# Two-layer macaron encoder on one core: the instruction order laid down with the builder's other machine model

## The chip, the core and the metric

The kernel runs on one core of one Trainium2 chip. Its time is that of one execution on the device in microseconds (us); several executions give a median. A core has five engines that each work through their own list of instructions strictly in order, and that wait for each other only where one needs the other's data or a buffer that it frees: PE (TensorE, matmuls, with its weight loads shown apart as PEld), DVE (VectorE), ACT (ScalarE), POOL (GpSimd) and SP (SyncE, which here only issues DMAs).

## What is computed

The reference applies two layers to x of 512 positions and 1024 channels, in fp32, and a last RMSNorm:

```python
x = x + 0.5 * swiglu(rmsnorm(x), gate1, up1, down1)       # hidden width 2816
h = rmsnorm(x); p = h @ w_in                               # 2048 columns
# A, 256 columns: centred means over 2, 4, 8, 16 positions minus the token, a map per group
# B, 256 columns: real part of a 2-D DFT over (positions, group channels), a linear map
# C, q, k, v of 4 heads: softmax(q1 k1) - lam * softmax(q2 k2), with a distance penalty,
#    times v, RMSNorm per head
x = x + concat(A, B, C) @ w_out
x = x + 0.5 * swiglu(rmsnorm(x), gate2, up2, down2)
```

## The kernel before

x lies in SBUF as eight tiles of 128 channels x 512 positions. Every fp32 factor is taken apart into a rounded part hi (ACT, L103) and the rest lo (DVE, in some steps POOL, L104); a product is three matmuls: hi with hi, and hi with lo both ways (L107 to L109 in general, L386 to L388 in the feed-forward products).

**Weights.** They come in blocks of 128 x 1024 by DMAs that SP issues (L158) into seven buffers named st. Some blocks are sums of two blocks of the weight matrix; there POOL issues a second DMA that adds to what lies in the buffer (L160), and another after a block has been used, which turns the buffer into the next sum (L175). `produce` makes hi and lo of a block, in four buffers each, and `operand` hands them out, three blocks ahead.

**Feed-forward block.** It has 11 units in three chunks of 4, 4 and 3. A unit computes two gate and two up tiles of 128 hidden channels with seven products instead of eight, over halves of the positions, accumulated in four PSUM banks qe, qa, qb, qg: `head` (qe, qa, then a copy q1 of qa, L395), `middle` (qb, qg; then y, v, w on DVE, L402 to L404; then qa again) and `tail` (qg again, qe again, then the SiLU products). In the program the tail of a unit stands behind the head of the next. A product is 24 matmuls. At a chunk's end come eight down products (banks dn), each of 24 (18) matmuls of 512 columns, added to x (L452). The norm's squares (ACT, L274), their sum (POOL, the last on DVE, L278) and the sum over channels on PE (bank ss, L254 and L255) run beside the first unit and are needed by its last step.

**Mixer.** Its steps are named in a list, ORDER (L44 to L48): `P` and `E` project q and k of a head and scale and split them (tq, tk at L474 and L475; qs, kh, kl at L480 to L485), `S01` is the scores of head 0 for the positions of block 1, `V0` and `V1` the values, `T` transposes, `X` weighs the values (bank AV), `Y` finishes a head, `GH` is a channel map of the Fourier part, `PL` the pooling part's map. A score step: two matmul pairs give scores in PSUM (S), DVE adds the distance penalty and takes the maximum in one instruction (L499), a small DVE instruction scales the maximum to nb (L503), ACT takes the exponential with its row sum (L504), DVE inverts the sums (L506) and scales (L507), one of three engines scales the first softmax (L509 is ACT's, L511 DVE's, L513 POOL's), and DVE subtracts the second (L514).

**What sets the order.** The program text gives only the order in which instructions are handed to the builder. The builder lays down each engine's list itself: it runs through the program with a model of the machine, takes what the model says is ready, and writes every engine's instructions in the order in which the model starts them. Priorities follow the program's order. All semaphores and waits come after that. The model's answer is thus fixed in the kernel: at run time an instruction whose inputs are late blocks everything behind it on its engine.

## Time and profile before

| | |
|---|---|
| median of 3 runs | 1875.59 us (1872.73 to 1879.64) |
| profiled execution | 1877.81 us |
| its span, first to last instruction | 1876.0 us |
| mean granted TensorE clock | 0.982 |
| HBM read | 261.09 MB, 140 GB/s over the span |
| DMA engines' share, POOL's queue and SP's | 29.1% and 27.7% |

One execution is profiled. A row of the timeline gives the start in us, the duration, the engine, the line, the operation, the tile written and those read, and in brackets how long the engine had been idle and who ended that. Matmuls overlap: a row's duration is longer than the distance to the next row. The granted clock is the share of full speed at which TensorE was allowed to run.

### The profile page before, as it was taken

To read this page: it belongs to the slowest core of one execution; us is meant where nothing else is said; L and a number is where in the kernel's file an instruction comes from. 1 tells how busy PE (TensorE), PEld (TensorE's weight loads), DVE (VectorE), ACT (ScalarE), POOL (GpSimd) and SP (SyncE) were. 2 spreads that over 40 slices of the span, in tenths; PEclk is the share of its full clock that TensorE was granted. 3 is DMA by queue.
4 is the path that set the end of the run, shared out by engine and by line. 5 is a ranking of instruction groups with operands and counts; after the bars stand their busy time and mean duration, and the time that the engine had idled before them with its cause. 6 is when DMAs were issued, how large, how long until landed. Compare 5 with 4: busy or idle time off the path is not lost.

```text
span 1876.0 us, 27955 instructions
## 1 busy us (share of the span) xinstructions
PE 1774.7 (95%) x11225; PEld 1603.5 (85%) x11225; DVE 1360.3 (73%) x1956; ACT 851.9 (45%) x1189; POOL 320.6 (17%) x282
## 2 busy tenths in 40 slices
PE   5899999999879999999999999999996989999997
PEld 4898989987668999989989899898775889899896
DVE  6675765789779874855798567478987897567474
ACT  6342533448545442534555234243773554244243
POOL 3101101032322101101031010113232220010101
PEclk9899999999989999999999999999998999999998
DMA  8666867532213866857678577573322267586561
GB/s 231 150 169 137 204 165 156 138 120 85 65 42 78 188 161 147 211 151 155 161 154 195 142 167 189 129 180 124 93 71 56 65 140 197 128 193 177 127 166 45
DMA packets 76738, 265.01 MB, mean 141 GB/s; under 512 B 8640, under 2 KB 10688, under 8 KB 76608
## 3 DMA queue, kind: packets, MB, share of 16 engines
q0 software_dynamic: 25344, 92.29, 29.1%
q1 hardware_dynamic: 48096, 167.25, 27.7%
q10 hardware_dynamic: 3168, 3.68, 0.7%
q8 instruction: 88, 1.44, 0.3%
q14 instruction: 42, 0.34, 0.1%
HBM read 261.09 MB, written 2.10 MB: 140 GB/s over the span
## 4 chain that ended last, share of the span: by engine, by line
PE 69%; DVE 12%; issue 7%; DMA 5%; ACT 5%; POOL 2%; SPq 0%; DVEq 0%; ACTq 0%; POOLq 0%
PE dn L107 7%; PE dn L108 7%; PE dn L109 7%; DMA st<-in_gu 5%; PE qg L386 4%; PE qg L387 4%; PE qg L388 4%; PE qe L386 3%; PE qe L387 3%; PE qe L388 3%; PE qa L388 3%; PE qa L386 3%; PE qa L387 3%; DVE lo L104 2%; ACT hi L103 2%
## 5 line engine op out<-in xcount | busy, mean ns | idle before, releaser
L103 ACT ACTIVATE hi<-st 128x1024 fp32r<-128x1024 f32 (+2 forms) x455 | 469.2, 1036 | 668.0 <-PE dn L108 214.8
L104 DVE TENSOR_TENSOR lo<-st,hi 128x1024 fp32r<-128x1024 f32 (+2 forms) x423 | 511.5, 1213 | 179.4 <-ACT hi L103 178.3
L108 PE MATMUL dn<-al,hi 128*128 128x512 f32 x704 | 274.6, 390 | 0.0
L109 PE MATMUL dn<-ah,lo 128*128 128x512 f32 x704 | 274.1, 389 | 0.0
L107 PE MATMUL dn<-ah,hi 128*128 128x512 f32 x704 | 272.1, 392 | 0.8
L175 POOL DMA_DIRECT2D st<-in_gu x132 | 120.7, 914 | 680.3 <-DVE lo L104 606.2
L386 PE MATMUL qe<-xh,hi 128*128 128x256 f32 x704 | 203.3, 289 | 20.0 <-ACT hi L103 10.3
L386 PE MATMUL qg<-xh,hi 128*128 128x256 f32 x704 | 201.3, 286 | 8.1 <-DVE w L404 7.7
L387 PE MATMUL qe<-xh,lo 128*128 128x256 f32 x704 | 202.6, 288 | 2.2 <-DVE lo L104 2.2
L388 PE MATMUL qe<-xl,hi 128*128 128x256 f32 x704 | 202.1, 287 | 1.8 <-DVE xl L104 1.8
L387 PE MATMUL qg<-xh,lo 128*128 128x256 f32 x704 | 200.8, 285 | 2.8 <-DVE lo L104 2.8
L388 PE MATMUL qg<-xl,hi 128*128 128x256 f32 x704 | 200.6, 285 | 0.0
L452 DVE SCALAR_TENSOR_TENSOR x<-dn,x 128x512 f32<-128x512 f32 x96 | 66.1, 689 | 163.2 <-PE dn L109 163.2
L107 PEld LDWEIGHTS dn<-ah,hi 128*128 128x128 f32 x704 | 131.3, 188 | 33.1 <-ACT ah L103 7.1
L386 PEld LDWEIGHTS qe<-xh,hi 128*128 128x128 f32 x704 | 137.9, 196 | 23.9 <-ACT hi L103 16.0
L108 PEld LDWEIGHTS dn<-al,hi 128*128 128x128 f32 x704 | 132.2, 188 | 29.0 <-DVE al L104 2.4
L109 PEld LDWEIGHTS dn<-ah,lo 128*128 128x128 f32 x704 | 132.2, 188 | 26.8
L386 PEld LDWEIGHTS qg<-xh,hi 128*128 128x128 f32 x704 | 136.4, 194 | 9.4 <-DVE w L404 7.6
L387 PEld LDWEIGHTS qe<-xh,lo 128*128 128x128 f32 x704 | 137.9, 196 | 4.0 <-DVE lo L104 3.1
L388 PEld LDWEIGHTS qe<-xl,hi 128*128 128x128 f32 x704 | 138.0, 196 | 2.4 <-DVE xl L104 2.0
L387 PEld LDWEIGHTS qg<-xh,lo 128*128 128x128 f32 x704 | 136.5, 194 | 3.0 <-DVE lo L104 3.0
L388 PEld LDWEIGHTS qg<-xl,hi 128*128 128x128 f32 x704 | 136.6, 194 | 0.0
(252 smaller groups left out, 3979.1 us busy)
## 6 DMA issues: line engine op xcount, KB each, us to landing
st<-in_gu SPq DMA_DIRECT2D x176, 512.0 KB, 4.5
st<-in_gu POOLq DMA_DIRECT2D x176, 512.0 KB, 5.6
st<-in_dn SPq DMA_DIRECT2D x64, 512.0 KB, 4.3
st<-in_dn SPq DMA_DIRECT2D x32, 384.0 KB, 3.3
st<-in_qk SPq DMA_DIRECT2D x16, 512.0 KB, 3.6
st<-in_wo SPq DMA_DIRECT2D x16, 512.0 KB, 3.7
st<-in_wv SPq DMA_DIRECT2D x8, 512.0 KB, 3.9
st<-in_wfa SPq DMA_DIRECT2D x8, 512.0 KB, 3.7
```

What stands on the lines that cost most here:

```text
L103: A.activation(hi, src, AF.Copy)
L104: (lo_eng or V).tensor_tensor(lo, src, f(hi), SUB)
L107: T.matmul(o, lh, rh, start=start, stop=False)
L108: T.matmul(o, lh, rl, start=False, stop=False)
L109: T.matmul(o, ll, rh, start=False, stop=stop)
L175: G.dma_start(t[:, 0:w], then, accum_op=ADD)
L386: T.matmul(o, wh[:, s], xh, start=start and p == 0 and z == 0, stop=False, **k)
L387: T.matmul(o, wl[:, s], xh, start=False, stop=False, **k)
L388: T.matmul(o, wh[:, s], xl, start=False, stop=stop and p == NK - 1 and z == 1, **k)
L452: V.scalar_tensor_tensor(X[m], b, 0.5, X[m], MUL, ADD)
```

## The change

One argument where the kernel's context is made:

```diff
@@ -855,7 +855,7 @@
         arrays[f"in_{name}"] = a
         args[name] = nc.dram_tensor(f"in_{name}", a.shape, F32, kind="ExternalInput").ap()
     args["out"] = nc.dram_tensor("out_t", (KT, P, S), F32, kind="ExternalOutput").ap()
-    with _tile.TileContext(nc) as tc:
+    with _tile.TileContext(nc, schedule_with_timeline_sim=True) as tc:
         build(tc, **args)
     r = _run(nc, [arrays], core_ids=[0])
```

The builder then orders the instructions with its other model of the machine, one that has times for queues and transfers. The instructions, their operands and the engine of each stay the same; PE has 11196 rows in both orders and ACT 1142. SP's list does not change at all. On PE, DVE, ACT and POOL many rows move, nearly everywhere. Three places:

ScalarE at the start. xg, xh and xo are parts of the input, hi of a weight block; q is the copy q1, and the rows sq are the norm's squares. Before:

```order
L103 ACTIVATE hi_260<-st_91 128x1024
L103 ACTIVATE xh_242<-xg_223 128x512
L103 ACTIVATE hi_290<-st_102 128x1024
L103 ACTIVATE hi_350<-st_132 128x1024
L395 ACTIVATE q_51_318<-qa_247 128x512
L274 ACTIVATE sq_320<-x_81 128x512
L274 ACTIVATE sq_322<-x_82 128x512
L274 ACTIVATE sq_325<-x_83 128x512
L274 ACTIVATE sq_328<-x_84 128x512
```

And now:

```order
L103 ACTIVATE hi_250<-st_95 128x1024
L103 ACTIVATE xh_242<-xg_223 128x512
L395 ACTIVATE q_51_318<-qa_247 128x512
L274 ACTIVATE sq_320<-x_81 128x512
L274 ACTIVATE sq_322<-x_82 128x512
L274 ACTIVATE sq_325<-x_83 128x512
L274 ACTIVATE sq_328<-x_84 128x512
L274 ACTIVATE sq_331<-x_85 128x512
L274 ACTIVATE sq_334<-x_86 128x512
L274 ACTIVATE sq_337<-x_87 128x512
L274 ACTIVATE sq_340<-x_88 128x512
L103 ACTIVATE hi_255<-st_95 128x1024
```

The squares and q1 stood behind the conversions of five weight blocks (hi_250, further up, to hi_350); now they stand behind one, and the other four follow them. On GpSimd the additions of these squares move in the same way: four of the six stand in one piece now, ahead of a DMA issue that stood between the first two.

VectorE in the score steps of the first mixer, first group (head 0 block 1, head 1 blocks 1 and 3). S0 and S1 are scores, mx maxima, rs the row sums of ACT's exponentials. Before:

```order
L499 ISA sc_334_4033,mx_327_4019<-S1_333_4030,al_104 128x512
L499 ISA mx_327_4019 128x1
L503 TENSOR_SCALAR nb_328_4020<-mx_327_4019 128x1
L499 ISA sc_340_4048,mx_335_4041<-S1_339_4045,al_104 128x512
L499 ISA mx_335_4041 128x1
L506 RECIPROCAL rc_322_4000<-rs_321_3999 128x2
```

And now:

```order
L499 ISA sc_342_4055,mx_335_4041<-S1_341_4052,al_104 128x512
L499 ISA mx_335_4041 128x1
L474 SCALAR_TENSOR_TENSOR tq_343_4063<-pp0_309_3925,y_293_3806 128x512
L475 TENSOR_TENSOR tk_344_4064<-pp1_310_3926,y_293_3806 128x512
L503 TENSOR_SCALAR nb_320_3998<-mx_319_3997 128x1 x2
L503 TENSOR_SCALAR nb_328_4020<-mx_327_4019 128x1 x2
L503 TENSOR_SCALAR nb_336_4042<-mx_335_4041 128x1 x2
L482 TENSOR_TENSOR qs_345_4067<-tq_343_4063,qs_345_4067 64x512
L483 TENSOR_TENSOR kl_347_4069<-tk_344_4064,kh_346_4068 64x512
L506 RECIPROCAL rc_322_4000<-rs_321_3999 128x2
```

The L503 of a tile stood behind the next reduction or the one after; now all six of the group stand behind all six reductions (the first row is the last of them) and behind the two scalings of the next head, and the reciprocals and L507 follow in one piece. The second group has its first four L503 in one piece too.

TensorE where the first down products of the first block meet the next chunk's first unit. dn_1304 is the second down product, dn_1336 and dn_1368 the third and fourth; qe_950 is the last product of a tail. Before:

```order
L388 MATMUL qe_950<-xl_243,hi_1119 128x256
L109 MATMUL dn_1304<-ah_842,lo_1190 128x512
L107 MATMUL dn_1304<-ah_804,hi_1189 128x512
L108 MATMUL dn_1304<-al_805,hi_1189 128x512
L109 MATMUL dn_1304<-ah_804,lo_1190 128x512
L107 MATMUL dn_1304<-ah_1083,hi_1189 128x512
L108 MATMUL dn_1304<-al_1084,hi_1189 128x512
L109 MATMUL dn_1304<-ah_1083,lo_1190 128x512
L107 MATMUL dn_1304<-ah_1045,hi_1189 128x512
L108 MATMUL dn_1304<-al_1046,hi_1189 128x512
L109 MATMUL dn_1304<-ah_1045,lo_1190 128x512
L107 MATMUL dn_1336<-ah_600,hi_1229 128x512
```

And now:

```order
L386 MATMUL qe_950<-xh_242,hi_1119 128x256
L387 MATMUL qe_950<-xh_242,lo_1120 128x256
L388 MATMUL qe_950<-xl_243,hi_1119 128x256
L107 MATMUL dn_1336<-ah_600,hi_1229 128x512
L108 MATMUL dn_1336<-al_601,hi_1229 128x512
L107 MATMUL dn_1368<-ah_600,hi_1267 128x512
L108 MATMUL dn_1368<-al_601,hi_1267 128x512
L109 MATMUL dn_1336<-ah_600,lo_1230 128x512
L107 MATMUL dn_1336<-ah_562,hi_1229 128x512
L108 MATMUL dn_1336<-al_563,hi_1229 128x512
L109 MATMUL dn_1336<-ah_562,lo_1230 128x512
```

Ten matmuls of the second down product stood between the tail's last product and the third down product. Now the second is done before the tail's end, the tail's last six matmuls (the last three are shown; ahead of them stands the last of qg_1088) come right ahead of the third, and the third and the fourth start together.

Two more kinds of move have no rows here. At the start of a feed-forward block the tail of the first unit stands behind the norm's sum (ss) and the head of the second unit, where its last two products stood around them before, and in the first chunk the middle of a unit stands wholly ahead of the tail of the unit before it. In the mixers the channel map GH stands behind 36 matmuls of the projection F where it stood behind 17, and the value products (V0, V1) are spread earlier between the scores.

## The prediction

> **What bounds the kernel now.** I read the page first: span, busy engines, the chain.
>
> ```profile
> span 1876.0 us, 27955 instructions
> ...
> PE 1774.7 (95%) x11225; PEld 1603.5 (85%) x11225; DVE 1360.3 (73%) x1956; ACT 851.9 (45%) x1189; POOL 320.6 (17%) x282
> ...
> PE 69%; DVE 12%; issue 7%; DMA 5%; ACT 5%; POOL 2%; SPq 0%; DVEq 0%; ACTq 0%; POOLq 0%
> ```
>
> TensorE is busy for 1774.7 of 1876.0 us, so all its pauses together are 101.3 us. The change issues the same instructions with the same operands. It can take away pauses, add pauses, and alter how long TensorE runs at a reduced clock after a pause, and nothing else. So I looked for the stretches in which TensorE pauses (busy time by stretch; the columns are start and length, then busy us of PE, its weight loads, DVE, ACT and POOL, then granted clock, DMA share, GB/s).
>
> ```profile
> 0.00:57.00 57.00, 32.75 (x169) 28.89 (x170) 36.41 (x60) 29.21 (x49) 16.93 (x22) 0.91 0.83 221
> 57.00:100.00 43.00, 38.66 (x304) 38.30 (x304) 31.27 (x39) 18.29 (x22) 6.08 (x7) 0.92 0.66 147
> 415.00:460.00 45.00, 42.45 (x198) 33.33 (x197) 41.92 (x113) 38.41 (x77) 11.17 (x7) 1.00 0.23 74
> 460.00:520.00 60.00, 50.08 (x223) 39.91 (x221) 46.53 (x89) 34.53 (x63) 21.77 (x14) 0.97 0.29 79
> 520.00:560.00 40.00, 31.54 (x148) 25.26 (x149) 31.52 (x71) 18.41 (x37) 7.63 (x4) 0.87 0.14 40
> ```
>
> The start loses 24.3 and 4.3 us. The first mixer loses 2.6, 9.9 and 8.5 us, with VectorE at 41.92 of 45 in the attention scores. The second mixer repeats it. The rest lies in short waits where a feed-forward block begins. So four places decide.
>
> **The start.** The page's chain within the first 60 us and ScalarE's timeline:
>
> ```profile
> 36.18 4.27 ACT L274 ACTIVATE sq<-x 128x512 f32<-128x512 f32 x8
> ```
> ```profile
> 25.22 5.61 DMA st<-in_gu
> ...
> 43.80 1.57 POOL sq L278
> ...
> 47.67 1.29 POOL sq L278
> 48.98 0.70 DVE sq L278
> ...
> 50.39 0.79 PE ss L254
> ```
>
> The eight squares of the norm stand behind five weight conversions, four of which wait for later DMAs, so they run at 36.18 us, and the sum over them on GpSimd, interleaved with DMA issues, ends at 48.96. After the change ScalarE does the squares behind only one weight conversion (22.61 us in this trace, below), so they end near 28.5 (an estimate: 22.61 + 1.06, a few conversions, 4.27), and GpSimd adds four of them in one go. TensorE's pauses there:
>
> ```profile
> 23.72 0.58 PE L386 MATMUL qe<-xh,hi 128*128 128x256 f32 x1 [9.79 <-ACT hi L103]
> ...
> 46.51 0.58 PE L387 MATMUL qg<-xh,lo 128*128 128x256 f32 x1 [2.79 <-DVE lo L104]
> 50.39 0.79 PE L254 MATMUL ss<-g,ones 128*128 128x512 f32 x1 [1.17 <-ACT g L103]
> 86.00 0.58 PE L386 MATMUL qg<-xh,hi 128*128 128x256 f32 x1 [4.34 <-DVE w L404]
> ```
> ```profile
> 22.61 1.06 ACT L103 ACTIVATE hi<-st 128x1024 fp32r<-128x1024 f32 x1 [7.21 <-DMA st<-in_gu]
> ```
> ```profile
> 50.00:52.00 2.00, 1.61 (x6) 1.52 (x7) 1.41 (x2) 0.34 (x1) 0.00 (x0) 0.50 0.69 86
> ...
> 54.00:56.00 2.00, 2.00 (x11) 2.00 (x11) 1.90 (x4) 0.00 (x0) 0.00 (x0) 0.50 0.53 213
> 56.00:58.00 2.00, 2.00 (x17) 2.00 (x17) 0.67 (x2) 1.06 (x1) 0.00 (x0) 0.91 0.00 0
> 88.00:90.00 2.00, 2.00 (x11) 2.00 (x10) 0.00 (x0) 0.00 (x0) 0.00 (x0) 0.50 0.12 47
> 90.00:92.00 2.00, 2.00 (x16) 2.00 (x16) 0.82 (x2) 0.80 (x1) 0.00 (x0) 0.88 0.00 0
> ```
>
> The 9.79 us belong to a DMA and stay. Gone are 2.79 + 1.17 and 4.34 = 8.3 us. Gone too is the reduced clock behind them: from 50.39 TensorE works at half speed until about 56.2 (0.91 in the last stretch means 0.36 us more at half), 5.8 us in which 2.9 are lost, and from 86.00 to about 90.5, 4.5 us with 2.2 lost. Together 13.4. Against it: the third unit's middle products now stand ahead of the second unit's tail (two products of 24 matmuls at about 0.12 us, 5.8 us sooner; 38.66 us for 304 in the second row above is 0.127, with the slow stretch in it), while the accumulating DMA that they need takes 5.61 us to land and the DMA engines are busy (0.83, 0.66 above). Between 0 and 5.8 us of that is a new wait; I take 3.5. And GpSimd's additions now fall beside VectorE's work on the first operands:
>
> ```profile
> 23.70 1.23 DVE L104 TENSOR_TENSOR lo<-st,hi 128x1024 fp32r<-128x1024 f32 x1 [6.93 <-ACT hi L103]
> ...
> 41.42 5.03 DVE L104 TENSOR_TENSOR lo<-st,hi 128x1024 fp32r<-128x1024 f32 x2 [1.52 <-ACT hi L103]
> ```
>
> Two such subtractions beside GpSimd's additions took 5.03 where 2 x 1.23 is 2.46: 2.6 us of stretch. At the start now it would delay the operands of the second product; between 0 and 2.6, I take 1.9. Term: -13.4 + 3.5 + 1.9 = **-8.0** (ends: -13.4 with both free; -3 with both dear and one more pause of 2 us).
>
> [...]
>
> **Mixers: the scores.** The rows of the second group of score tiles, then ScalarE's exponentials and copies, then TensorE's wait behind them:
>
> ```profile
> 437.94 0.69 DVE L499 CUSTOM_DVE_ANT_0 sc<-S,al 128x512 f32<-128x512 f32 x1
> ...
> 456.08 0.75 DVE L514 SCALAR_TENSOR_TENSOR sc<-sc,rc,sc 128x512 f32<-128x512 f32 x1
> ```
> ```profile
> 425.55 0.71 ACT L504 ACTIVATE sc<-sc,nb 128x512 f32<-128x512 f32 x1
> ...
> 426.25 0.71 ACT L504 ACTIVATE sc<-sc,nb 128x512 f32<-128x512 f32 x1
> ...
> 430.30 0.62 ACT L480 ACTIVATE qs<-tq 64x512 fp32r<-64x512 f32 x1
> ```
> ```profile
> 455.39 0.87 PE L522 MATMUL T<-ident,sc 128*128 128x128 f32 x6 [1.12 <-DVE sc L514]
> ```
>
> Before, the little L503 that an exponential waits for stands right behind its reduction (L499), so ScalarE's exponentials overlap VectorE's reductions. After, the six L503 of the first group stand behind all six reductions and the two q/k scalings. The six exponentials, 0.70 apart by the rows, then start when the reductions are done: 4.2 us in which VectorE has little, then ScalarE's four q/k copies (0.62 each) and the two L509 that its last additions wait for. Walking the new order with those durations, I get group two's first reduction at 440.5 instead of 437.94 (+2.6) and, with its own first L503 behind four reductions instead of two (two more, 1.3 us, and half a us of pairing), the last L514 4.4 later than 456.08. TensorE has no filler left: the value projection, which filled here, is done earlier. Later in the mixer the channel-map product comes behind 19 more matmuls, and the pool product is given more work ahead of it:
>
> ```profile
> 525.00 0.80 PE L108 MATMUL PL<-g,g 128*128 128x512 f32 x1 [5.46 <-DVE g L104]
> ```
>
> The 19 matmuls x 0.23 (rows below) = 4.4 us of delay on the one side and up to 5.46 us of filled pause on the other nearly cancel; I take +0.6 for the pair. Term: 2 x (4.4 + 0.6) = **+10** (ends: 0 if TensorE finds other work; 2 x 10.7, rival C).
>
> **Feed-forward entries.**
>
> ```profile
> 615.38 0.36 PE L386 MATMUL qe<-xh,hi 128*128 128x256 f32 x1 [1.55 <-DVE v L403]
> 616.43 0.58 PE L387 MATMUL qe<-xh,lo 128*128 128x256 f32 x1 [0.69 <-DVE lo L104]
> ...
> 1560.72 0.39 PE L386 MATMUL qg<-xh,hi 128*128 128x256 f32 x1 [1.48 <-DVE w L404]
> ```
>
> At the three later blocks the first unit's tail is moved behind the norm's sum and the second unit's head, so its wait for v (1.55) and for the next operand (0.69) have 5.8 us of other products ahead of them and go; in the last block also the 1.48 for w. That is -2.2 to -3.7 each. The same move asks for accumulated operands 5.8 us sooner, as at the start: 0 to +3. I take -2 each. Term: **-6** (ends -9 and +3).
>
> **Down products.** Between two pieces of a down product, TensorE used to have ten matmuls of an older down product in reserve; now six of a unit's tail follow there and then the next two down products at once.
>
> ```profile
> L103 ACT ACTIVATE hi<-st 128x1024 fp32r<-128x1024 f32 (+2 forms) x455 | 469.2, 1036 | 668.0 <-PE dn L108 214.8
> L104 DVE TENSOR_TENSOR lo<-st,hi 128x1024 fp32r<-128x1024 f32 (+2 forms) x423 | 511.5, 1213 | 179.4 <-ACT hi L103 178.3
> ```
> ```profile
> 139.40 0.39 PE L107 MATMUL dn<-ah,hi 128*128 128x512 f32 x1
> 139.63 0.40 PE L108 MATMUL dn<-al,hi 128*128 128x512 f32 x1
> ```
>
> A weight operand needs 1.04 (ScalarE) + 1.21 (VectorE) us after its buffer comes free, and the buffer of the first new operand comes free with the last tail product ahead of those six. Six matmuls at 0.12 are 0.7 us, so its first half is 0.4 late with semaphores; then four matmuls at 0.23 use first halves alone (0.9 us) against 1.21 for the second half, and the next operand is 0.6 behind. That is 1.0 to 1.75 us per block, before there was no pause; four blocks, I take 1.25 each. Term: **+5** (0 if the converting engines run ahead, +7).
>
> **Sum.** -8 + 10 - 6 + 5 = +1. The profiled execution took 1877.81 us (its span 1876.0 and 1.8 around it) and would take 1878.8; it stands 2.2 above the median of the runs, 1875.59, so the forecast is **1876.6 us**. About 0.5%, 9.4 us, is what a measurement of this kernel can tell from no change.
>
> **The rivals.**
> A, the order hardly matters: each engine still waits for the same last arrivals, most moves lie among instructions that waited anyway, and TensorE's 95% stay: 1875.6. For it speaks that three quarters of the span is dense; against it that the quoted pauses sit at in-order instructions that do move.
> B, the pauses at the start and the entries go whole and the mixers hide their delay: -13.4 - 9 + 0 + 5 = -17.4, 1858.2. For it speaks that the start's 13.4 are rows; against it DMA shares of 0.83 and 0.66 there and VectorE's 41.92 of 45 in the scores. It decides when the mixer costs under 2 us each.
> C, slower by VectorE's new order in the scores: the 4.4 is not caught up, the channel map's 4.4 come on top instead of being filled, and the longer pause puts TensorE on half clock for 4.5 us, of which it loses 1.9 to 2.2. 4.4 + 4.4 + 1.9 = 10.7 per mixer, 21.4 for two; with the other terms as taken -8 + 21.4 - 6 + 5 = +12.4, 1888.0. It counts as slower from 9.2 us per mixer on (-9 + 2 x 9.2 = 9.4). For it speaks VectorE's fill there; against it the 5.46 us pause in which a delay can vanish.
>
> **How the numbers follow.** Forecast 0.32 (its own range 1868 to 1885), A 0.10, B 0.30, C 0.28. A and the forecast lie within 0.5%: 0.42. The range goes from B, 1858, to 4 us beyond C, 1892, for dear ends of the entries or down products coming with it; a tenth is left out on each side.
>
> **What would show it.** Right at the start: squares near 25 us, the norm's sum matmul near 41 instead of 50.39, no half clock at 50 to 56, more DMA wait between 50 and 85. Right in the mixers: last L514 of the first three heads about 4 us later counted from the mixer's first L499, and a longer pause ahead of the transposes. Right at the down products: pauses of 0.3 to 0.6 us ended by ScalarE's hi. The forecast is wrong if TensorE's pauses over 415 to 560 don't change, or if the first 100 us gain under 3 or over 14.

## The result, and the profile after

The changed kernel takes 1968.14 us (median of 4 runs, 1965.83 to 1970.07) where the kernel before takes 1877.48 (median of 4 as well; the table further up has the first 3): the ratio is 1.0485, 95% interval 1.0464 to 1.0507. It is 4.8% slower. The forecast was no change, 1876.6 us, with 1892 as the upper end.

The page of the changed kernel (span, busy time, chain):

```profile
span 1964.1 us, 27955 instructions
...
PE 1804.7 (92%) x11225; PEld 1621.8 (83%) x11225; DVE 1355.1 (69%) x1956; ACT 851.3 (43%) x1189; POOL 310.5 (16%) x282
...
PE 60%; DVE 16%; DMA 8%; issue 8%; ACT 7%; POOL 1%; ACTq 0%; DVEq 0%; POOLq 0%; SPq 0%
```

The work is the same. TensorE pauses for 159.4 us instead of 101.3. It is also busy for 30.0 us longer, since it runs more of the work at a reduced clock (granted 0.965 on the mean instead of 0.982). The same stretches as before, put where the stages lie now (columns as in the prediction):

```profile
0.00:57.00 57.00, 41.09 (x232) 36.83 (x233) 41.75 (x67) 33.64 (x53) 17.56 (x23) 0.94 0.88 240
57.00:100.00 43.00, 42.14 (x351) 41.93 (x351) 35.49 (x44) 20.45 (x25) 6.03 (x7) 1.00 0.82 192
408.00:453.00 45.00, 38.51 (x166) 29.95 (x165) 35.08 (x105) 33.65 (x68) 11.96 (x7) 0.95 0.22 71
453.00:513.00 60.00, 44.23 (x188) 36.26 (x187) 40.04 (x63) 29.08 (x52) 15.47 (x11) 0.81 0.24 64
513.00:573.00 60.00, 44.71 (x190) 34.87 (x188) 37.22 (x93) 22.52 (x43) 10.79 (x5) 0.83 0.11 36
```

The first 100 us have become denser (83.2 us of TensorE work instead of 71.4). The mixer has become thinner in every part, and VectorE with it: in the scores it is busy for 35 of 45 us where it was busy for 42. An engine that does less per us and is waited for more is held up by something else. The starts of some instructions in both traces say how much each stage has won or lost:

| end of a stage (the instruction's start) | before, us | after, us | this stage |
|---|---|---|---|
| first chunk of the first block (last L452 of it) | 169.78 | 158.42 | -11.4 |
| the first block (last L452) | 392.21 | 384.60 | +3.7 |
| first mixer, head 3's output (L543) | 571.36 | 589.32 | +25.6 |
| second block's first chunk | 730.89 | 760.48 | +11.6 |
| the second block | 952.96 | 985.50 | +2.9 |
| third block's first chunk | 1082.90 | 1123.75 | +8.3 |
| the third block | 1306.44 | 1351.25 | +4.0 |
| second mixer, head 3's output | 1484.33 | 1556.55 | +27.4 |
| fourth block's first chunk | 1642.53 | 1727.72 | +13.0 |
| the fourth block | 1860.69 | 1948.25 | +2.4 |

The pauses of TensorE in the first mixer, in the changed kernel's timeline, one row for each of the long ones:

```profile
452.13 1.12 PE L522 MATMUL T<-ident,sc 128*128 128x128 f32 x4 [3.20 <-DVE sc L514]
...
486.38 0.80 PE L254 MATMUL ss<-osh,ones 128*128 128x512 f32 x1 [6.52 <-ACT osh L103]
...
508.04 0.58 PE L107 MATMUL GH<-g,g 128*128 128x256 f32 x1 [8.67 <-ACT g L103]
...
533.74 0.79 PE L107 MATMUL PL<-g,g 128*128 128x512 f32 x1 [8.88 <-ACT g L103]
```

Before, these waits were 1.12, 1.52, 3.90 and 2.70 us. The last three end with ScalarE. What ScalarE does ahead of the second of them, after and before:

```profile
482.05 0.63 ACT L103 ACTIVATE yh<-yo 128x512 fp32r<-128x512 f32 x1 [4.10 <-DVE yo L543]
...
482.59 2.04 ACT L103 ACTIVATE th<-T 128x512 fp32r<-128x512 f32 x4
...
485.09 0.58 ACT L536 ACTIVATE osq<-AV 128x512 f32<-128x512 f32 x1
485.70 0.63 ACT L103 ACTIVATE osh<-osq 128x512 fp32r<-128x512 f32 x1
```
```profile
478.41 0.63 ACT L103 ACTIVATE yh<-yo 128x512 fp32r<-128x512 f32 x1 [0.42 <-DVE yo L543]
```

yh is the output of head 0, at the end of that head's chain: sum on TensorE, then ten steps on ScalarE and VectorE up to yo. Head 1's osq needs nothing of it, but it stands behind yh and th in ScalarE's list. In the changed kernel the chain ends later, ScalarE stands still for 4.10 us, and so does all that is behind.

### The profile page after: what moved, and what is told of

The parts are those of the page before. It is cut to its first block, busy times and chain, and to the rows that moved or that the text cites. A ratio compares the mean times of both kernels' runs of the same rounds, so it can differ in the third digit from the quotient of the medians.

```text
span 1964.1 us, 27955 instructions
## 1 busy us (share of the span) xinstructions
PE 1804.7 (92%) x11225; PEld 1621.8 (83%) x11225; DVE 1355.1 (69%) x1956; ACT 851.3 (43%) x1189; POOL 310.5 (16%) x282
## 4 chain that ended last, share of the span: by engine, by line
PE 60%; DVE 16%; DMA 8%; issue 8%; ACT 7%; POOL 1%; ACTq 0%; DVEq 0%; POOLq 0%; SPq 0%
DMA st<-in_gu 8%; PE dn L107 7%; PE dn L109 6%; PE dn L108 6%; DVE lo L104 3%; PE qg L387 3%; PE qg L388 3%; PE qg L386 3%; PE qe L386 3%; PE qe L387 3%; PE qe L388 3%; PE qa L387 3%; PE qa L386 3%; PE qa L388 3%; ACT hi L103 3%
## 5 line engine op out<-in xcount | busy, mean ns | idle before, releaser
L452 DVE SCALAR_TENSOR_TENSOR x<-dn,x 128x512 f32<-128x512 f32 x96 | 66.0, 688 | 132.2 <-PE dn L109 132.2
```

What stands on the lines that cost most here:

```text
L452: V.scalar_tensor_tensor(X[m], b, 0.5, X[m], MUL, ADD)
```

## The experiments

For every experiment the order is spliced. The program is laid out with the one model and with the other; then each engine's list is taken from one, and in the places of some chosen instructions it gets the same instructions in the order of the other list. A last build has every engine's list pinned by edges that keep issue order and add no wait. The instructions stay the same. Where an instruction belongs (place) is the step of the program that made it: "F1 chunk 0" is the first block's first chunk, "M1 Y0" the step Y0 of the first mixer.

```diff
+    base, where = make(False)[2:]        # each engine's list, old model
+    other = make(True)[2]                # the same, new model
+    lay = {}
+    for e in base:
+        moved = iter([n for n in other[e] if PICK(e, where[n])])
+        lay[e] = [next(moved) if PICK(e, where[n]) else n for n in base[e]]
+    nc, arrays = make(False, lay)[:2]
...
+            for queue in lay.values():
+                for n, m in zip(queue, queue[1:]):
+                    tc.add_manual_dep(traced[m], n, behind, reason="order")
```

Only PICK differs between most experiments, so that line is their diff. Differences below are against the median of before on the same chip, 1874.8 to 1876.6 us. The first theory was: the order alone is the cause, and each stage's loss is its own, the mixers' above all.

**e1, everything in the new order.**

```diff
+    return True
```

> The kernel before, built with its own model, but with every engine's list pinned to the order of the changed kernel. Theory (the order of the instructions alone is the cause): 1968 us within 4. Rival (the buffers that the other model's build hands out, or anything else in that build, have a share): clearly under 1968, towards 1877.

1962.6 us, ratio 1.046 (1.0438 to 1.0482), +86.5: 1.4 us under the theory's lower end, with an interval that overlaps that of the changed kernel. The order of the lists does it; for a share of the buffers no more than the 0.3% between the two medians is left.

**e2, the start alone.**

```diff
+    return place in ("set up", "F1 chunk 0", "F1 down 0")
```

> The order of before everywhere, that of the changed kernel only for the set up and the first block's first chunk of units and down products. By the traces that stretch ends 11.4 us sooner in the changed kernel (158.42 against 169.78). Theory (a stretch's gain or loss is its own): 1866 us, between 1863 and 1869. Rival (the gain is given back at the next wait for data): 1874 to 1878.

1863.8 us, ratio 0.9938 (0.9919 to 0.9957), -12.3. The gain at the start is real and stays to the end.

**e3, both mixers, and e4, the third chunks.**

```diff
+    return place[0] == "M"
```

> The order of before everywhere, that of the changed kernel only for the instructions of the two mixers. By the traces the mixers, from the end of the block ahead to the last head's output, are 25.6 and 27.4 us longer in the changed kernel. Theory (mixers carry the main loss by themselves): 1930 us, between 1922 and 1942. Rival (the mixers are longer because what runs beside them, the next block's weights and first unit, is laid out differently): under 1905.

1947.1 us, ratio 1.0388 (1.0359 to 1.0417), +71.0: more than the theory's 53. In the traces a part of the mixers' cost had been booked at the next block's first chunk, which waits for their last output.

```diff
+    return place[-1] == "8"
```

> The order of before everywhere, that of the changed kernel only for the third chunk (units and down products) of the four feed-forward blocks. By the traces these are 3.7, 2.9, 3.7 and 1.8 us longer, 12.1 together. Theory (the waits of 0.4 to 1.2 us ahead of the down products are these): 1889 us, between 1885 and 1893. Rival (they come from what the next mixer's order pulls in): under 1881.

1889.8 us, ratio 1.0069 (1.0044 to 1.0093), +13.7. e4's first block, TensorE ahead of down products:

```profile
359.79 0.50 PE L107 MATMUL dn<-ah,hi 128*128 128x512 f32 x1 [0.46 <-ACT hi L103]
...
366.29 1.21 PE L107 MATMUL dn<-ah,hi 128*128 128x512 f32 x4 [1.22 <-ACT ah L103]
```

The first row is a wait for hi of the kind and size that the prediction described (0.3 to 0.6), though its place was the first chunk. The second it did not have: the next down products now start before the last hidden tile is split.

**e12, the third block's first chunk** (told here because it closes the sum).

```diff
+    return place[:2] == "F3" and place[-1] == "0"
```

> The order of before everywhere, that of the changed kernel only for the first chunk of the third feed-forward block. The prediction said 2 us less; by the traces that stretch is 8.3 us longer. Theory (operands asked for sooner, waits for hi, xh and q): 1885, between 1881 and 1888. Rival (what stands ahead of it in the changed kernel makes it late): 1872 to 1878.

1884.0 us, ratio 1.0047 (1.0034 to 1.006), +8.5. The four parts add up to -12.3 + 71.0 + 13.7 + 8.5 = 80.9 of e1's 86.5 us. So most of the losses are local and add. No run took the first chunks of the second and fourth blocks alone. Counted from the end of the block ahead they end at 375.88 and 376.47 us in the changed kernel and at 371.89 and 372.45 in e3, which leaves these chunks in the old order: some of the missing 5.6 may lie there.

**e5 and e6, the two halves of the mixers.** E is the list of steps up to X0.

```diff
+    return place[0] == "M" and place[3:] in E
```

> The order of before everywhere, that of the changed kernel only for the first half of each mixer's step list (from the projections to the weighting of head 0's values, X0; the scores of heads 0 to 2 are in it). By the traces, from the norm's sum to head 0's sum the changed kernel is 7.7 and 7.3 us longer. Theory (the scores carry the smaller part): 1891 us, between 1884 and 1898. Rival (the scores' order carries most of the mixers' 71 us): over 1920.

1888.8 us, ratio 1.007 (1.0055 to 1.0085), +12.2.

```diff
+    return place[0] == "M" and place[3:] not in E
```

> The order of before everywhere, that of the changed kernel only for the second half of each mixer's step list (from the last scores of head 2 and Y0 to the output projections W0 to W3). Theory (the bare waits of 6.5, 8.7 and 8.9 us and the slow clock behind them are here): 71 - 15 = 56 us over before, 1932 us, between 1920 and 1942. Rival (they come from the first half's delay): under 1900.

1933.4 us, ratio 1.0308 (1.0293 to 1.0323), +56.7. Four fifths of the mixers' loss lie behind the scores.

**e7, the second half, TensorE's list alone.**

```diff
+    return place[0] == "M" and engine == "PE" and place[3:] not in E
```

> As e6, but only TensorE's list is taken from the changed kernel in the second half of the mixers; the other engines keep the order of before. Theory (TensorE's list alone makes the waits, because filling matmuls are used up ahead of an item that waits): at least two thirds of what e6 adds, 1913 us or more. Rival (the lists of ScalarE and VectorE make the operands late): under 1895.

1921.2 us, ratio 1.0243 (1.0227 to 1.0258), +44.5: 78% of e6. With ScalarE's and VectorE's lists as before, TensorE's order is enough.

**e8, the softmax rows alone.**

```diff
+    return place[0] == "M" and engine != "PE" and place[3] == "S"
```

> The order of before everywhere, that of the changed kernel only for the score steps' instructions on VectorE, ScalarE and GpSimd (among them the small L503 that now stand behind all reductions); TensorE as before. The prediction's price was 4.4 us per mixer: 1885 us. Theory now (it holds, as the scores' own part): between 1880 and 1890. Rival (exponentials and reductions keep up, the scores lose through TensorE's list): 1874 to 1879.

1901.8 us, ratio 1.0149 (1.013 to 1.0168), +25.2: nearly three times the 8.8 us that the prediction's price gives for two mixers, and outside both readings. Its pauses in the first mixer:

```profile
441.07 0.50 PE L496 MATMUL S<-kh,qs 128*128 128x512 f32 x1 [2.38 <-DVE mx L499]
...
492.28 0.79 PE L254 MATMUL ss<-osh,ones 128*128 128x512 f32 x1 [4.90 <-ACT osh L103]
```

It is also twice e5's 12.2, but the two hold unlike parts: e8 has all the score steps, e5 only those up to X0. Both have changed the same ones ahead of the first transposes (first L522). Counted from the end of the block ahead, in the first and the second mixer, these begin at 56.6 and 56.6 us before, at 63.1 and 63.1 in e5 and at 63.4 and 62.4 in e8. So far the order of VectorE, ScalarE and GpSimd alone makes as much delay as e5 has with all its lists. Head 0's output (L543) then comes at 85.4 before, at 91.3 and 90.8 in e5 and at 96.1 and 95.1 in e8: the rest of e8's loss arises behind the first transposes. Whether it would be smaller with TensorE's list of the same steps no run shows, so a part done alone is a price for that part in the other order, and not its share of the whole.

**e9, four matmuls moved.**

```diff
+    return engine == "PE" and place[0] == "M" and place[3:] in ("Y0", "P3", "Y1", "A")
```

> The order of before, and in TensorE's list four instructions moved to where the changed kernel has them: the second matmul (L255) of the sums for heads 0 and 1, in each mixer, goes from behind 3 and 0 matmuls of the next projection to behind 21 and 20. Theory (a late sum delays ScalarE and VectorE's chain for the head, ScalarE's list stands behind that chain, and TensorE meets the lack at the next sum and at the channel map): 18 and 20 matmuls x 0.228 = 4.1 and 4.6 us, 17.4 for two mixers, and up to 8 us of slow clock: 1894 to 1902. Rival (the chain has room): under 1882.

1892.0 us, ratio 1.0095 (1.0082 to 1.0108), +16.5, where 17.4 had been worked out from the moves alone; the 8 us allowed for the slow clock did not come, which puts the time 2 us under the theory's range. The rows of TensorE in e9, first the two halves of head 0's sum, then head 1's, then the channel map; behind them ScalarE:

```profile
464.46 0.39 PE L254 MATMUL ss<-osh,ones 128*128 128x512 f32 x1
...
469.45 0.39 PE L255 MATMUL ss<-osl,ones 128*128 128x512 f32 x1
...
486.49 0.80 PE L254 MATMUL ss<-osh,ones 128*128 128x512 f32 x1 [6.04 <-ACT osh L103]
...
505.97 0.58 PE L107 MATMUL GH<-g,g 128*128 128x256 f32 x1 [5.96 <-ACT g L103]
```
```profile
482.38 0.63 ACT L103 ACTIVATE yh<-yo 128x512 fp32r<-128x512 f32 x1 [5.49 <-DVE yo L543]
...
482.92 2.04 ACT L103 ACTIVATE th<-T 128x512 fp32r<-128x512 f32 x4
```

Before, the two halves stand 0.9 us apart:

```profile
465.57 0.39 PE L254 MATMUL ss<-osh,ones 128*128 128x512 f32 x1
...
466.47 0.39 PE L255 MATMUL ss<-osl,ones 128*128 128x512 f32 x1
```

Now they stand 5.0 us apart. Those 4.1 us pass through head 0's chain to yh, through ScalarE's list to th and osq, and back to TensorE as the wait of 6.04. TensorE lost nothing where the matmul was moved: it was busy with the next projection.

**e10, the channel map's second half.**

```diff
+    return engine == "PE" and place[0] == "M" and place[3:] in ("GH", "S30", "S32", "F")
```

> The order of before, and in TensorE's list only the second half of the channel map (GH, 8 matmuls) moved from behind 17 to behind 36 matmuls of the projection F, in each mixer. The prediction had 4.4 us of delay per mixer for it, given back elsewhere. Theory now (it is not on the chain, since the wait is at GH's first half): within 4 us of before. Rival (the prediction's price without the return): 1885.

1882.5 us, ratio 1.0045 (1.0028 to 1.0062), +7.0. My theory of this step fell. The pooling product's first wait, before and in e10:

```profile
518.58 0.50 PE L107 MATMUL PL<-g,g 128*128 128x512 f32 x1 [2.70 <-ACT g L103]
```
```profile
518.18 0.79 PE L107 MATMUL PL<-g,g 128*128 128x512 f32 x1 [6.18 <-ACT g L103]
```

That is 3.5 us more, and the second mixer has the same 6.18: together 7.0, most of the 4.4 us per mixer that the prediction had booked. But the profiled execution is the fastest of e10's six, 1877.3 us of 1877.3 to 1890.0, and hardly longer than before. In it the wait ahead of the channel map (GH) is 1.23 us instead of the 3.90 in the trace of before. That need not be the move's doing: in e2, which leaves the mixers alone, the wait is 3.89 in the first and 1.23 in the second. Set against e2's second mixer, head 3's output comes 3.5 and 2.2 us later in e10's two (179.7 and 178.4 us after the block ahead, against 176.2). So the trace shows the delay too, though less of it in the second mixer.

**e11, the four matmuls put back in the changed order.**

```diff
-    return True
+    return not (engine == "PE" and place[0] == "M" and place[3:] in ("Y0", "P3", "Y1", "A"))
```

> The changed order everywhere, except that the same four matmuls stand where before has them. Theory (they carry much of the mixers' loss): 17 to 25 us under the pinned changed order's 1962.6, so 1938 to 1946. Rival (other waits of the changed order take over): over 1956.

1969.5 us, ratio 1.0503 (1.0486 to 1.052): no gain, if anything a loss. In the changed kernel the lists of ScalarE and VectorE themselves hold head 0's chain back. The rows where the chain begins, on ScalarE (L227) and VectorE (L242), and then L242 before:

```profile
470.43 0.73 ACT L509 ACTIVATE sc<-sc,rc 128x512 f32<-128x512 f32 x1 [0.55 <-DVE rc L506]
471.05 0.58 ACT L227 ACTIVATE v<-ss 128x512 f32<-128x512 f32 x1
```
```profile
471.19 0.75 DVE L514 SCALAR_TENSOR_TENSOR sc<-sc,rc,sc 128x512 f32<-128x512 f32 x1 [0.55 <-ACT sc L509]
471.85 0.42 DVE L242 TENSOR_SCALAR y<-v 128x512 int32<-128x512 int32 x1
```
```profile
468.60 0.43 DVE L242 TENSOR_SCALAR y<-v 128x512 int32<-128x512 int32 x1
```

L227 stands behind the L509 of head 2's scores and so behind the exponentials, and L242 behind the subtraction that waits for this L509. Before, L242 ran ahead of both subtractions of that group. The sum in time does not help as long as these come first. The four matmuls are enough to lose 16.5 us in the old order, but not the one cause in the new.

**e13 and e17, the reduced clock.** Fillers (ones times ones, 128 columns, into the bank that the next real matmul overwrites) ahead of items that wait; w is the number.

```diff
+        def warm(b, n):
+            EXTRA.extend(T.matmul(b[:, 0:P], ones, ones, start=True, stop=True).ins.name for _ in range(n * WARM[0]))
...
-                    b = bank("GH")
+                    b = bank("GH"); warm(b, w * (z == 0))
```

> The pinned changed order, with small filling matmuls (ones by ones, 128 columns, written to the bank that the next real matmul overwrites) ahead of four items in each mixer: 56 ahead of head 1's sum, 76 ahead of the channel map and ahead of the first pooling product, 24 ahead of the second. They fill the pauses of 6.5, 8.7, 8.9 and 3.2 us and compute nothing that is kept. Theory (the slow clock behind the pauses is a cost of its own: granted clock 0.91 and 0.85 over 400 to 600 us against 1.00 and 0.93): 10 us or more per mixer come back, 1943 or less, and the granted clock there is near 1. Rival (what follows a pause waits anyway): within 6 us of 1962.6.

1963.9 us, ratio 1.0487 (1.0446 to 1.0528). Not clean: in the first mixer the fillers ahead of head 1's sum held it back, by 6 us.

> As e13 without the fillers ahead of head 1's sum, which in e13 began late, ran at half clock and held the sum back by 6 us: 76 ahead of the channel map, 72 ahead of the first pooling product, 20 ahead of the second. Theory (behind these pauses the slow clock costs about 5 us per mixer, by e13's stretch from head 1's output to head 2's, 62.9 against 67.7 us): 1950 to 1956. Rival (the slow clock costs nothing, what follows waits anyway): 1960 to 1966.

1964.4 us, ratio 1.0483 (1.0457 to 1.0509). e17 and then e1, 500 to 600 us:

```profile
500.00:600.00 100.00, 94.33 (x505) 79.16 (x504) 63.60 (x135) 35.80 (x67) 16.55 (x11) 0.93 0.19 48
```
```profile
500.00:600.00 100.00, 75.28 (x330) 59.84 (x329) 63.05 (x131) 33.08 (x63) 18.13 (x12) 0.88 0.18 47
```

TensorE is busy for 94.33 of 100 us instead of 75.28 and its clock is higher, while VectorE and ScalarE do little more in the same 100 us (63.60 against 63.05, 35.80 against 33.08). The kernel's time shows no cost of the slow clock of its own; a few us per mixer can't be excluded. In e13's second mixer, where the fillers did not hold the sum back, head 3's output comes 6.4 us sooner than in e1 (197.7 instead of 204.1 us after the block ahead), and of that 1.9 are left at the end of the next block's first chunk. So the clock was higher where the pauses were filled (granted 0.93 instead of 0.88 over these 100 us); the kernel's time, 1964.4 us against e1's 1962.6, didn't depend on it as far as these runs can tell.

**e14 and e16, the useful parts alone.**

```diff
+    return place in ("set up", "F1 chunk 0", "F1 down 0") or engine == "PE" and place[3:] in ("PL0", "X2", "S31", "S33")
```

> The order of before, that of the changed kernel for the start (as e2), and in TensorE's list two matmuls per mixer moved: the second and third of the first pooling product stand behind 20 matmuls of head 2's values and head 3's scores, as in the changed kernel. Theory (the 5.46 us pause of before at that place is filled): 4 to 5 us per mixer under e2's 1863.8, 1854 to 1857. Rival (the scores that come sooner wait elsewhere): 1862 to 1866.

1861.8 us, ratio 0.993 (0.9903 to 0.9957). It beats both kernels, as e2 does; the two can't be told apart. The two pooling products in e14:

```profile
504.26 0.79 PE L107 MATMUL PL<-g,g 128*128 128x512 f32 x1 [2.72 <-ACT g L103]
...
516.32 0.79 PE L107 MATMUL PL<-g,g 128*128 128x512 f32 x1 [4.88 <-ACT g L103]
```

The pause of 5.46 us inside the first product is filled. The second, which waited 1.45 us, now waits 4.88: most of a filled pause is only moved where the same chain feeds the next item.

> e14, and filling matmuls as in e13 ahead of the same four items, fewer of them (8, 30, 18 and 8), since the pauses of before are 1.5, 3.9, 2.7 and 1.45 us there. They compute nothing that is kept. Theory of the clock: the slow stretches of before at 500 to 560 us (granted clock 0.87 over 40 us) go, 2 to 5 us per mixer: 1846 to 1852. Rival: no change from e14.

1865.5 us, ratio 0.9954 (0.9934 to 0.9975), for e14's order with fillers put in as in e13: the fillers gain nothing here either.

**e15 and e18, the end of the mixers.**

```diff
+    return engine == "PE" and place[0] == "M" and place[3:] in "PL1 T3 W0a Y2 FG0 W1a FG1 X3 FD1 FD0 W0b W1b Y3 W2 W3".split()
```

> The order of before, and TensorE's list of the changed kernel only for the mixers' last steps (second pooling product, head 3's transposes, Fourier products, output projections). e7's 44.5 us less the 16.5 of e9 and the 7 of e10 leave 21. Theory (the output projections are given in another order, so the next block's inputs come late): 1890 to 1900. Rival (the remainder is the pooling product and the sum of delays): 1874 to 1880.

1893.1 us, ratio 1.0099 (1.0067 to 1.0131), +18.1.

```diff
+    return engine == "PE" and place[0] == "M" and place[3:] in "W0b W1b Y3 W2 W3".split()
```

> The order of before, and in TensorE's list only the late parts of the output projections (W0b, W1b, W2, W3, with head 3's sum among them) in the changed order: 19 matmuls of the third projection more stand ahead of the last parts of the first two. Theory (x of the first two projections comes 19 x 0.228 = 4.3 us late, and the next block's first unit waits for it, the 5.81 us of e15): 13 to 18 us over before, 1888 to 1893. Rival (e15's loss comes from the Fourier products): under 1880.

1888.2 us, ratio 1.0076 (1.006 to 1.0093), +13.5, most of e15's. In e18 the next block's first unit waits:

```profile
598.05 0.58 PE L386 MATMUL qe<-xh,hi 128*128 128x256 f32 x1 [5.81 <-ACT xh L103]
```

At that place the wait was 2.28 us before:

```profile
598.28 0.39 PE L386 MATMUL qe<-xh,hi 128*128 128x256 f32 x1 [2.28 <-ACT xh L103]
```

The last parts of the first two projections stand behind 19 more matmuls of the third, so four tiles of x, their norm and their splits come late. The 3.5 us more, in each of two mixers, and a new wait of 0.80 us at 589.83 make 8.7 of the 13.5. Of e7's 44.5 us, 16.5 (e9), 7.0 (e10) and 18.1 (e15) make 41.6.

## Why the prediction was wrong

**The start: the size right, the parts only in part.** The term was -8.0, with ends of -13.4 and -3; e2 measures -12.3. The rows that answer to those of before, on ScalarE, GpSimd, VectorE and TensorE:

```profile
23.19 4.26 ACT L274 ACTIVATE sq<-x 128x512 f32<-128x512 f32 x8
```
```profile
24.41 5.65 POOL L278 TENSOR_TENSOR sq<-sq,sq 128x512 f32<-128x512 f32 x4
```
```profile
31.72 7.03 DVE L104 TENSOR_TENSOR lo<-st,hi 128x1024 fp32r<-128x1024 f32 x4 [7.58 <-ACT hi L103]
```
```profile
43.99 0.40 PE L254 MATMUL ss<-g,ones 128*128 128x512 f32 x1
```
```profile
50.00:52.00 2.00, 2.00 (x19) 2.00 (x18) 1.90 (x4) 1.54 (x2) 0.86 (x1) 1.00 1.13 371
```

The squares run at 23.19 instead of 36.18, the sum's matmul at 43.99 without a wait, and the half clocks at 50 and at 86 us are gone (granted 1.00 at both), with the pause of 4.34 ahead of the second. Of the new DMA wait that I took at 3.5 there is 0.86 (for a lo at 74.40, TensorE's only wait from 50 to 85 us); the stretch of VectorE beside GpSimd's other two additions (3.82 us from 33.86) came (7.03 for four where 4 x 1.23 is 4.9: 2.1, against 1.9).

So -13.4 + 0.9 + 2.1 is -10.4, near what was measured (a slip of 0.1 aside: 0.36 us behind 56.00 is 56.4, and not 56.2). But that is in part luck, since things that the sum didn't have work against each other. The pause of 9.79 us that would "stay" is more than half gone: products of qa with xo now stand ahead, with waits of 1.83 and 1.82 us, and that matmul waits 0.73. e2's -12.3 also holds 1.5 us of new waits at the first chunk's down products (below). And behind a pause of 3.00 us for hi a slow stretch comes sooner, in the changed kernel:

```profile
34.00:36.00 2.00, 2.00 (x12) 2.00 (x11) 2.00 (x2) 0.54 (x1) 1.92 (x3) 0.50 0.61 70
36.00:38.00 2.00, 2.00 (x11) 2.00 (x11) 2.00 (x2) 0.00 (x0) 1.68 (x1) 0.50 1.02 223
```

Here 11 or 12 matmuls run in 2 us where the row of 50 us has 19. GpSimd's four additions in one go (5.65 us from 24.41) fell into 7.58 us in which VectorE had nothing to do, so these four stretched nothing there.

**The scores: right in kind, a little low.** I had 4.4 us per mixer; e5 has 12.2 for two. That exponentials start late and TensorE has no filler shows in the wait of 3.20 ahead of the transposes. The last L514 ahead of them comes 36.5 us after the mixer's first L499 instead of 33.4: 3.1 later, where about 4 had been forecast. e8 has the same delay at the first transposes without TensorE's list, so the other engines' order is enough to make it, as the prediction said. What share L503 has in it no run shows.

**The rest of the mixers: here it failed.** The step was "The 19 matmuls x 0.23 (rows below) = 4.4 us of delay on the one side and up to 5.46 us of filled pause on the other nearly cancel; I take +0.6 for the pair." Measured, the channel map's delay costs 7.0 for two mixers (e10), and the filled pause returns nothing that can be told (e14). And the sum left out what cost most: the sums' second halves (16.5, e9) and the output projections (13.5, e18), both in the order of TensorE and neither priced. e6's 56.7 stand where the sum had 1.2. The reason is one: I went through TensorE's pauses and asked what new order would do to each, and took a matmul moved behind other useful matmuls as free. In this part of the mixers TensorE isn't what sets the time. By e9 it is VectorE's and ScalarE's chain per head, and a matmul on that chain costs its delay nearly in full (16.5 of 17.4), however busy TensorE is meanwhile. Rival C had the right side and two of the costs about right (8.8 for the scores and 8.8 for the channel map, measured 12.2 and 7.0); it lacked the sums and the output projections as the forecast did, and so had a third of the mixers' 71.0.

**Entries: wrong side.** I had -2 each; e12 measures +8.5 for the third block, 5.6 of it within that chunk in its trace (135.5 us instead of 129.9). The waits of the first unit for v and for the next operand, 1.56 and 0.68 there, are gone as forecast. But others come later in the same chunk: 1.51 for v of another unit, at 1061.94 us in the changed kernel, and at 1035.99 and 1037.25 us 1.72 and 0.87 for a weight operand whose DMA ScalarE had waited for, near the dear end of that price. And there is a new one for q. In the changed kernel, ScalarE and then TensorE:

```profile
997.34 1.98 ACT L103 ACTIVATE hi<-st 128x1024 fp32r<-128x1024 f32 x2
...
999.75 0.57 ACT L395 ACTIVATE q<-qa 128x512 f32<-128x512 f32 x1
```
```profile
1000.38 0.39 PE L386 MATMUL qa<-xh,hi 128*128 128x256 f32 x1 [2.53 <-ACT q L395]
```

The copy q1, which the next product on qa waits for, now stands behind two weight conversions in ScalarE's list where it stood behind one; in e12 the wait is there too, 2.54. The gain that I had counted, operands with other products ahead of them, was paid with conversions that are asked for sooner and stand in the way.

**Down products: right at the place that was priced, and absent from the sum at another.** The rows of that term, and its count of one place in each of four blocks, are those of the first chunks. In the changed kernel's first block:

```profile
112.66 0.50 PE L107 MATMUL dn<-ah,hi 128*128 128x512 f32 x1 [0.97 <-ACT ah L103]
...
122.18 0.50 PE L107 MATMUL dn<-ah,hi 128*128 128x512 f32 x1 [0.48 <-ACT hi L103]
```

The wait for hi is there with the size it should have; the larger one, for ah, was not foreseen. Over the four blocks these and a wait of 0.38 for lo in two of them make 6.7 us, where I had 5. The third chunks were not in the sum, and they cost 13.7 (e4). In e4's trace the waits shown above make 6.5 in four blocks, and at the third block's entry the first matmul waits longer for x:

```profile
958.86 0.58 PE L386 MATMUL qe<-xh,hi 128*128 128x256 f32 x1 [5.72 <-ACT xh L103]
```

Before, the longest wait there was 1.83 us (at 953.10, for xl), so 3.9 more. What makes the other 3.3 of the 13.7 stays open, as do the 5.6 us between e1 and the sum of its parts.

## What to carry to other kernels

When an order changes, ask first which chain sets the time in each stage; there, price a moved instruction by how much later its result reaches the chain, and not by whether its own engine stays busy. In-order lists pass a delay on to work that has nothing to do with it (in e9 head 0's sum came 4.1 us late, and TensorE's wait ahead of head 1's sum grew from 1.52 to 6.04): look at what stands behind the waiting instruction on every engine it goes through. An order from another model need not be taken whole: splice stage by stage, keep what gains (here the start, 0.6%), and leave the rest.

## What was not expected of the hardware

In e13's first mixer the 56 fillers of 128 columns ahead of head 1's sum, which began after a pause of 2.15 us, took 10.3 us, 0.18 each, at a granted clock of 0.59; in its second mixer the same 56 began after 1.58 us and took 0.11 each. So here fillers that began late were themselves slow and held back, by 6 us, what they were to speed up. And the kernel's time was the same, as far as the runs can tell, with granted clock 0.93 and TensorE 94% busy over 500 to 600 us as with 0.88 and 75%. At the very start the clock column does not say it all: from 24 to 28 us the changed kernel runs 11 matmuls in each 2 us, as in the half clock at 36 us, while the column has 1.00.
